# Softmax with temperature: from eight small tile buffers to a ring of large blocks with a row maximum

## The chip, the cores and the metric

The kernel runs on one core of a Trainium2 chip. The metric is the device time of one execution in microseconds (us), lower is better. Before the change, ten runs have a median of 319.7 us and lie between 319.55 and 319.8.

Five engines matter for reading it. ACT (ScalarE) computes exponentials, DVE (VectorE) reduces and multiplies, SP (SyncE) only issues transfers, and PE and POOL do next to nothing here. Transfers between the chip's main memory (HBM) and its on-chip memory (SBUF, 128 partitions) are issued from the queue of an engine (SP's and ACT's in this case) and carried by 16 DMA engines.

## The reference

`x` is 32 x 512 x 1024 float32, 67.1 MB. The temperature is 0.5.

```python
scaled = x / temperature
shifted = scaled - np.max(scaled, axis=-1, keepdims=True)
exp_x = np.exp(shifted)
return (exp_x / np.sum(exp_x, axis=-1, keepdims=True)).astype(np.float32)
```

It is a softmax over rows of 1024 elements, and there are 16384 rows. All of `x` must be read once and all of the result written once, 134.2 MB together.

## The kernel before, in words

The rows are taken 512 at a time: 128 partitions, with K = 4 consecutive rows in each. One such tile is 2 MiB, 16 KiB in each partition, and the four rows of a partition lie next to each other in HBM too. There are 32 tiles, and one loop goes over them (`for it, (g0, K) in enumerate(sched)`). A pool of eight buffers (`data`) holds the tiles; a tile is computed in place, so its buffer is taken from the start of its load to the end of its store.

For each tile the loop issues, in this order:

- the load, from SP's queue (line 47);
- four exponentials on ACT (line 52), one per row of the partition. Each computes exp(scale * x) and also leaves the sum of its row in `sums`. The maximum is not subtracted;
- one reciprocal of the four sums on DVE (line 59);
- four multiplications on DVE (line 61), each with its row's reciprocal;
- the store, from ACT's queue (line 70). For the last four tiles the store is cut in two halves, one from ACT's queue (line 67) and one from SP's (line 68).

The waits are not written out. The tile framework derives them from the buffers: a load waits for the store of the tile that had its buffer eight tiles earlier, an exponential waits for the load, a reciprocal for the exponentials, a store for the multiplications. Each engine works through its own instructions in program order, so SP's queue holds 32 loads with the four last half stores behind them, and ACT's queue holds the exponentials with the stores between them. The store of tile n stands in ACT's queue where the loop puts it, three exponentials into the next tile (the compiler's order), so that ACT need not stand still for DVE.

Of the kernel before, what the change touches and what calls it, by code (L numbers as in the profile page):

```python
# [1 line left out]

# [4 lines left out]


@with_exitstack  # L10
def kernel(
    ctx: ExitStack,
    tc: tile.TileContext,
    x: bass.AP,
    temperature: bass.AP,
    out: bass.AP,
):
    nc = tc.nc
    scale = 1.0 / float(temperature)

    P = 128
    xf = x.flatten_outer_dims()
    of = out.flatten_outer_dims()
    n, d = xf.shape
    nrowgroups = n // P

    K_MAIN = 4
    SPLIT_LAST = 4
    sched = []
    g = 0  # L30
    while g < nrowgroups:
        k = min(K_MAIN, nrowgroups - g)
        sched.append((g, k))
        g += k
    ntiles = len(sched)

    data = ctx.enter_context(tc.tile_pool(name="data", bufs=8))
    stats = ctx.enter_context(tc.tile_pool(name="stats", bufs=16))

    for it, (g0, K) in enumerate(sched):  # L40
        rows = P * K
        r0 = g0 * P
        xv = xf[r0 : r0 + rows, :].rearrange("(p k) d -> p (k d)", p=P, k=K)
        ov = of[r0 : r0 + rows, :].rearrange("(p k) d -> p k d", p=P, k=K)

        xtile = data.tile([P, K, d], mybir.dt.float32)
        nc.sync.dma_start(out=xtile.rearrange("p k d -> p (k d)"), in_=xv)  # L47

        sums = stats.tile([P, K], mybir.dt.float32)
        recip = stats.tile([P, K], mybir.dt.float32)  # L50
        for j in range(K):
            nc.scalar.activation(  # L52
                xtile[:, j, :],
                xtile[:, j, :],
                mybir.ActivationFunctionType.Exp,
                scale=scale,
                accum_out=sums[:, j : j + 1],
            )
        nc.vector.reciprocal(recip, sums)  # L59
        for j in range(K):  # L60
            nc.vector.tensor_scalar_mul(  # L61
                xtile[:, j, :], in0=xtile[:, j, :], scalar1=recip[:, j : j + 1]
            )

        if it >= ntiles - SPLIT_LAST and K > 1:
            h = K // 2
            nc.scalar.dma_start(out=ov[:, :h, :], in_=xtile[:, :h, :])  # L67
            nc.sync.dma_start(out=ov[:, h:, :], in_=xtile[:, h:, :])
        else:
            nc.scalar.dma_start(out=ov, in_=xtile)  # L70


# [1 line left out]
_INS = ['x', 'temperature']  # L74
_OUTS = [((32, 512, 1024), 'float32')]
#: Inputs that are plain numbers.
_NUMBERS = {'temperature': 0.5}


# [26 lines left out]
```

## Time and profile before

| | |
|---|---|
| median of 10 runs | 319.7 us |
| the profiled execution's own time | 320.02 us |
| its span in the profile | 318.1 us |
| ACT busy | 138.0 us (43%) |
| DVE busy | 93.4 us (29%) |
| exponential, 128 x 1024, line 52 | 128 times, mean 1044 ns |
| multiplication, 128 x 1024, line 61 | 128 times, mean 749 ns |
| reciprocal, 128 x 4, line 59 | 32 times, mean 178 ns |
| bytes moved | 67.11 MB read, 67.11 MB written, mean 422 GB/s |
| load of 2 MiB, issue to landing | median 31.2 us, least 7.8 us |
| store of 2 MiB from ACT's queue, issue to landing | median 24.3 us |

The span is what the profiler sees between the first and the last instruction; the time of an execution is some 1.9 us longer, and the profiled execution is itself 0.3 us above the median. Busy times are sums over one execution. In the row of 40 digits each digit is the busy share of one fortieth of the span (about 8 us), in tenths. The chain that ended last is followed back from the end: at each step to what released the waiting work. A line of the windows table gives a stretch in us from the span's start, its length, the busy time and number of instructions of DVE, ACT and POOL, the granted TensorE clock, the DMA engines' busy share, and the rate in GB/s. A line of the waits gives who waited for what, and then the total in us, how many times, and the longest.

### The profile page before, as it was taken

The numbers are of one execution on the slowest core, as the hardware profiler recorded it, in microseconds if no ns is written. First come the engines' busy times: TensorE is split into PE (matmuls) and PEld (weight loads), VectorE is DVE, ScalarE is ACT, GpSimd is POOL, SyncE is SP. The second block draws the span as 40 slices with busy tenths as digits, with TensorE's granted clock in tenths as the row PEclk, the third lists the DMA queues.
The fourth block names the chain that finished last, engine by engine and source line by source line (L and its number), as shares of the span: only waits on it lengthen the run. The fifth ranks groups of instructions, "written<-read, shape, count | busy, mean of one in ns | idle before, by whom it ended". The sixth has DMA issues, their size and how long they took to land.

```text
span 318.1 us, 636 instructions
## 1 busy us (share of the span) xinstructions
DVE 93.4 (29%) x160; ACT 138.0 (43%) x257; POOL 0.2 (0%) x4
## 2 busy tenths in 40 slices
DVE  0352333212300517631333213333123003733300
ACT  1875334553321739655334553345543106852500
POOL 0000000000000000000000000000000000000000
DMA  8999999999999999999999999999999999999996
GB/s 291 433 398 429 429 429 428 431 429 439 433 437 433 428 431 429 429 429 431 429 431 434 437 433 433 431 429 431 429 429 431 429 433 433 439 433 419 427 427 265
DMA packets 9797, 134.26 MB, mean 422 GB/s; under 512 B 1088, under 2 KB 1088, under 8 KB 1088
## 3 DMA queue, kind: packets, MB, share of 16 engines
q1 hardware_dynamic: 5184, 71.31, 52.9%
q10 hardware_dynamic: 4608, 62.92, 46.2%
q14 instruction: 5, 0.04, 0.0%
HBM read 67.11 MB, written 67.11 MB: 422 GB/s over the span
## 4 chain that ended last, share of the span: by engine, by line
DMA 91%; ACT 1%; SPq 1%; DVE 1%; issue 0%; DVEq 0%; ACTq 0%
DMA xtile<-in_x_dram 55%; DMA out_dram<-xtile 36%; ACT xtile L52 1%; SPq L47 1%; DVE xtile L61 1%; DVEq L101 0%; ACTq L67 0%; DVE recip L59 0%; ACTq L52 0%; ACTq L70 0%
## 5 line engine op out<-in xcount | busy, mean ns | idle before, releaser
L52 ACT ACTIVATE xtile<-xtile 128x1024 f32<-128x1024 f32 x128 | 133.6, 1044 | 159.6 <-DMA xtile<-in_x_dram 158.4
L61 DVE TENSOR_SCALAR xtile<-xtile,recip 128x1024 f32<-128x1024 f32 x128 | 87.7, 749 | 1.1
L59 DVE RECIPROCAL recip<-sums 128x4 f32<-128x4 f32 x32 | 5.7, 178 | 206.7 <-ACT xtile L52 206.7
L52 ACT ACTIVATION_READ_ACCUMULATOR xtile<-xtile 128x1 f32 x128 | 23.9, 187 | 0.0
L52 ACT ACT_TABLE_LOAD x1 | 1.3, 1283 | 0.7 <-PEq L87 0.7
L87 POOL MEMSET const-bfloat16-1.0<- 128x1 bf16 x1 | 0.1, 101 | 0.0
L87 POOL MEMSET const-uint8-127<- 128x1 uint8 x1 | 0.1, 101 | 0.0
L87 POOL MEMSET const-float32-0.0<- 128x1 f32 x1 | 0.1, 98 | 0.2 <-issue 0.2
L87 POOL MEMSET const-float32-1.0<- 128x1 f32 x1 | 0.1, 98 | 0.0
## 6 DMA issues: line engine op xcount, KB each, us to landing
xtile<-in_x_dram SPq DMA_DIRECT2D x32, 2048.0 KB, 31.2
out_dram<-xtile ACTq DMA_DIRECT2D x28, 2048.0 KB, 24.3
out_dram<-xtile ACTq DMA_DIRECT2D x4, 1024.0 KB, 22.8
out_dram<-xtile SPq DMA_DIRECT2D x4, 1024.0 KB, 14.9
```

The source lines that it names most:

```text
L47: nc.sync.dma_start(out=xtile.rearrange("p k d -> p (k d)"), in_=xv)
L52: nc.scalar.activation(xtile[:, j, :], xtile[:, j, :], mybir.ActivationFunctionType.Exp, scale=scale, accum_out=sums[:, j : j + 1],)
L59: nc.vector.reciprocal(recip, sums)
L61: nc.vector.tensor_scalar_mul(xtile[:, j, :], in0=xtile[:, j, :], scalar1=recip[:, j : j + 1])
L87: nc = _bacc.Bacc("TRN2", target_bir_lowering=False, num_devices=1)
```

## The change

The kernel's loop is replaced by lists that are written out by hand, and the framework's waits by semaphores (counters on which an engine can wait).

- **Blocks.** Nine loads in place of 32: seven of 16 rows per partition (8 MiB, 64 KiB in each partition) and two of 8 rows (4 MiB). Ten stores in place of 36: six of 16 rows, four of 8.
- **Ring.** One buffer of 48 rows per partition (192 KiB), in which blocks 0 to 8 lie at rows 0, 16, 32, 0, 16, 32, 0, 16 and 24. A load waits for the store of what lay in its place: loads 3, 4, 5, 6 wait for stores 0, 1, 2, 3, and loads 7 and 8 both for store 4. A semaphore for each load and each store carries these waits.
- **Row maximum.** For each group of four rows per partition DVE finds the maxima (one reduction of 128 x 4 x 1024, line 91) and multiplies them by minus the scale (line 101); the exponential on ACT (line 109) takes the result as its bias.
- **Order on DVE.** For g from 0 to 32: maximum and bias of group g, then reciprocal (line 122) and four multiplications (line 128) of group g - 1. So the last group of a block is multiplied behind the maximum of the next block's first group.
- **Order on ACT.** The exponentials of group g, then a store (line 149) if group g - 1 was the last of one. The store waits for that group's multiplications.
- **Order on SP.** The nine loads (line 142), then waits for the stores that are left. No store is issued from SP any more.

```diff
+LOADS = [16] * 7 + [8] * 2
+STORES = [[16]] * 6 + [[8, 8]] + [[8]] * 2
+RING = 48
+GROUP = 4
...
-    data = ctx.enter_context(tc.tile_pool(name="data", bufs=8))
-    stats = ctx.enter_context(tc.tile_pool(name="stats", bufs=16))
...
-        nc.sync.dma_start(out=xtile.rearrange("p k d -> p (k d)"), in_=xv)
...
-        nc.vector.reciprocal(recip, sums)
-        for j in range(K):
-            nc.vector.tensor_scalar_mul(
-                xtile[:, j, :], in0=xtile[:, j, :], scalar1=recip[:, j : j + 1]
...
+    def maximum(g):
+        i, s, r, k = groups[g]
+        if g == 0 or groups[g - 1][0] != i:
+            nc.vector.wait_ge(loaded[i], 16)
+        nc.vector.tensor_reduce(
+            out=top[:, r : r + k],
+            in_=ring[:, s : s + k, :],
+            axis=mybir.AxisListType.X,
+            op=extreme,
+        ).then_inc(topped, 1)
+
+    def shift(g):
+        i, s, r, k = groups[g]
+        nc.vector.wait_ge(topped, g + 1)
+        nc.vector.tensor_scalar_mul(
+            bias[:, r : r + k], in0=top[:, r : r + k], scalar1=-scale
+        ).then_inc(biased, 1)
+
+    def exponential(g):
+        i, s, r, k = groups[g]
+        nc.scalar.wait_ge(biased, g + 1)
+        for a in range(k):
+            ins = nc.scalar.activation(
+                ring[:, s + a, :],
+                ring[:, s + a, :],
                 mybir.ActivationFunctionType.Exp,
+                bias=bias[:, r + a : r + a + 1],
                 scale=scale,
-                accum_out=sums[:, j : j + 1],
+                accum_out=sums[:, r + a : r + a + 1],
             )
+        ins.then_inc(summed, 1)
...
+    def load(i):
+        nonlocal free_to
+        s, r, k = places[i], first[i], LOADS[i]
+        for n, (l, s1, r1, k1) in enumerate(parts):
+            if l < i and s1 < s + k and s < s1 + k1 and n > free_to:
+                for b in range(free_to + 1, n + 1):
+                    nc.sync.wait_ge(stored[b], 16)
+                free_to = n
+        nc.sync.dma_start(out=ring[:, s : s + k, :], in_=dram(xf, r, k, i)).then_inc(
+            loaded[i], 16
+        )
+
+    def store(n):
+        l, s, r, k = parts[n]
+        nc.scalar.wait_ge(scaled, part_end[n])
+        nc.scalar.dma_start(out=dram(of, r, k, l), in_=ring[:, s : s + k, :]).then_inc(
+            stored[n], 16
+        )
+
+    free_to = -1
+    with tc.tile_critical():
+        for i in range(len(LOADS)):
+            load(i)
+        for b in range(free_to + 1, len(parts)):
+            nc.sync.wait_ge(stored[b], 16)
+
+        for g in range(len(groups) + 1):
+            if g < len(groups):
+                exponential(g)
+            for n in range(len(parts)):
+                if part_end[n] == g:
+                    store(n)
+
+        for g in range(len(groups) + 1):
+            if g < len(groups):
+                maximum(g)
+                shift(g)
+            if g > 0:
+                invert(g - 1)
+                divide(g - 1)
```

`invert` and `divide` are the reciprocal and the four multiplications of a group, on the ring's rows, with a wait on `summed` and on `inverted` ahead of them and an increment of `scaled` behind the last.

## The prediction

> **What bounds the kernel now.** I read the page's head and slices first, then the chain that ended last, then the queue's own waits, then short windows at both ends. Head, slices and queues:
>
> ```profile
> span 318.1 us, 636 instructions
> DVE 93.4 (29%) x160; ACT 138.0 (43%) x257; POOL 0.2 (0%) x4
> ...
> DMA  8999999999999999999999999999999999999996
> ...
> HBM read 67.11 MB, written 67.11 MB: 422 GB/s over the span
> ```
>
> No engine is half busy, but the DMA engines are full in every slice between the first and the last. The chain agrees: nine tenths of it is DMA.
>
> ```profile
> DMA 91%; ACT 1%; SPq 1%; DVE 1%; issue 0%; DVEq 0%; ACTq 0%
> DMA xtile<-in_x_dram 55%; DMA out_dram<-xtile 36%; ACT xtile L52 1%; SPq L47 1%; DVE xtile L61 1%; DVEq L101 0%; ACTq L67 0%; DVE recip L59 0%; ACTq L52 0%; ACTq L70 0%
> ```
>
> So the time is bytes over rate. 134.2 MB in some 310 us is about 430 GB/s, and windows show that rate whether loads run alone (8 to 16 us), both kinds run (128 to 192), or stores run alone (304 to 312):
>
> ```profile
> 8.00:16.00 8.00, 2.92 (x5) 6.85 (x13) 0.00 (x0) 1.00 1.00 430
> ...
> 128.00:192.00 64.00, 21.65 (x38) 30.28 (x58) 0.00 (x0) 1.00 1.01 432
> ...
> 304.00:312.00 8.00, 0.00 (x0) 0.00 (x0) 0.00 (x0) 1.00 1.01 429
> ```
>
> In the trace's packet records a 16 KiB packet takes 611 ns on its engine and an 8 KiB one 309 ns: 7 ns for the packet itself plus 604 ns per 16 KiB. Each engine carries 480 and 64 of them: 480 x 0.611 + 64 x 0.309 = 313.1 us. The other 5 us of the span are start and end. The only way to be slower is to leave the DMA engines empty. The queue's waits say how near that is:
>
> ```profile
> SPq L47 <- DMA out_dram<-xtile: 228.7, 24, 17.0
> ```
>
> Loads already wait for stores to free buffers, all the time, and it costs nothing: eight 16 KiB buffers mean that when one store lands, others are still in flight. What a transfer costs on an **empty** queue is seen only at the start. The first load is issued at 0.73, and the first bytes move after 1.7:
>
> ```profile
> 1.50:1.70 0.20, 0.00 (x0) 0.20 (x1) 0.00 (x0) 1.00 0.00 0
> 1.70:1.90 0.20, 0.00 (x0) 0.20 (x1) 0.00 (x0) 1.00 2.71 573
> ...
> 0.00:8.00 8.00, 0.00 (x0) 1.28 (x1) 0.20 (x4) 1.00 0.81 293
> ...
> DMA to landing us min/median/max: 7.8/31.2/48.4
> ```
>
> That is 1.0 us from issue to first byte. By 8.0 us 2.34 MB have moved, 5.45 us at 430 GB/s, so the effective start is 2.55: 0.8 us more are lost while the flow builds up. And that load took 7.8 us to land for 8 x 0.611 = 4.9 us of packets: 2.9 us of fixed cost on the slowest engine, of which about 0.35 lies after its last packet.
>
> **What the Trainium skill says.** "DMA: Bandwidth & Descriptors", section "Issuing engines are not separate DMA queues": SP's and ACT's transfers interleave on the same 16 engines; the windows agree (430 alone, 432 together). Same page, "Queues, rings and completion order": each engine serves the queues in turn, packet by packet; I take it that a load and a store in flight together get half each, which no row here shows singly. Same page, "Anatomy of one DMA": waits are held by the issuing sequencer, so a queue whose next transfer is unissued has nothing to run. "VectorE: DVE Perf Modes", the perf-mode tier table: a reduction handles one element per cycle; its price is below.
>
> **The change, part by part.**
>
> *Row maximum and bias.* 32 reductions of 128x4096 and 32 tiny multiplications are added on DVE. No such row exists. The skill's page gives about 150 fixed cycles and 0.96 GHz: (4096 + 150) / 0.96 = 4.42 us, an estimate; its other figure, 58 cycles, gives 4.33. The kernel's own multiplication has a pitch of 0.685 us for 1024 elements at two per cycle, which 150 fits ((512 + 150) / 0.96 = 0.69) and 58 does not; I take 4.45 with the wait, bounds 3.5 and 5.5. The small operations cost 0.2 each, as the reciprocal's step does (12.81 to 13.02). A group of four rows now costs DVE 4.45 + 0.2 + 0.2 + 2.75 (four multiplications, 13.02 on) = 7.6 us, in total 243 us instead of 93. This stays under the 9.7 us of transfers per group, so it does not bound by rate, but it sits in every buffer's round trip. ACT's work per group stays 4.16 us (four at a 1.04 pitch; its bias is taken at nothing, since ACT has 3 us to spare per group).
>
> *Longer transfers.* A partition's run grows from 16 to 64 KiB. If packets grow with it, an engine has 7 x 8 + 2 x 8 load packets and 6 x 8 + 4 x 8 store packets, 152 instead of 544: 392 x 7 ns = 2.7 us saved. If they don't, 0. I take 2.7.
>
> *Stores behind the next group.* The last multiplication of a block stands on DVE behind the maximum of the **next** block's first group, which waits for that block's load. So store n needs load n+1 landed plus 4.65 + 2.95 + 0.3 = 7.9 us. ACT's wait on the multiplications stands behind that group's exponentials and ahead of the next group's; DVE finishes about 3 us after ACT was released, ACT needs 4.2, so it costs nothing.
>
> *The ring.* Three 8 MiB blocks instead of eight of 2 MiB, and load n+3 waits for the whole of store n. A block is 8 packets of 2.42 us per engine, 19.4 us alone, 38.8 us when it shares with another. The walk, by hand:
>
> Load 0 lands at 22.5 (issued at 0.95, 0.2 later than now for the entry of the ordered section, + 1.0 + 0.8 + 19.4 + 0.35), the others by 61. Store 0 needs five maxima and four groups' multiplications: 22.5 + 5 x 4.65 + 4 x 2.95 = 57.6. Later blocks follow at 4 x 7.6 = 30.4 us: store 1 at 88.3 (with some 0.3 for hand-over). But store 0, which shares only with load 2's rest, is through at 80.3. **First gap**: nothing is in flight, load 3 is issued at 80.7, first byte 1.0 later, 0.8 to build up: 2.2 us. Load 3 then leads store 1 by 6.8 us; both finish their 38.8 us at 121.3, the load ahead, landed at 114.4. Store 2 is issued 7.9 later, 122.3; store 1 has already ended. **Second gap.** The rule: a round has a gap unless the load leads its store by 7.9 + 1.0 = 8.9 us or more. Walked on like this, the leads of the four rounds behind store 1 to store 4 come out as 6.8, about 0, 4.6 and 2.2 us, so with the first there are five dry ends (stores 0 to 4, at 80, 121, 162, 203, 244 us). From 245 on loads and stores of eight rows overlap; the last store is issued near 310 while the one before runs to 314.5, so the tail adds nothing.
>
> A gap costs 2.2 us by the mean over engines, 2.9 if the slowest engine pays in full, 1.4 if the build-up belongs to the program's start only. I take 2.3. **Sum: 318.1 + 5 x 2.3 - 2.7 = 326.9 us of span.** Fewer issues (19 for 68, 0.33 us each) were hidden behind full queues and count nothing. The profiled execution took 320.02, 1.9 above its span; the median shown, 319.7, is 1.6 above. With 1.6: **328.5 us**. With 1.4 per gap 324.0; with 2.9 and no packet saving 334.2.
>
> **Rivals.** (1) *Fewer gaps*: round 1 is only 2.1 us from the lead that closes its gap, so a different start could break the pattern. With two gaps: 318.1 + 4.6 - 2.7 + 1.6 = 321.6. Against: the first gap has 8 us of margin, and each later one is followed by a load and store starting nearly together. (2) *No gaps, faster*: if the reduction ran at two elements per cycle, (150 + 2048) / 0.96 = 2.3 us, a block would take 21.8 us, store 1 would be out before store 0 is through, and only the packet saving remains: 318.1 - 2.7 + 1.6 = 317.0. It decides at a reduction of about 3.2 us; the page's one element per cycle speaks against it. (3) *DVE becomes the bound*: at 6.5 us per maximum a group costs 9.7, and waiting for loads and computing no longer overlap; the same walk ends at 346, time 347.6. It begins to hurt from 5.5 (333 of span). Nothing in the trace shows DVE slowed by ACT or DMA. (4) *Long rows move slower*: 2% on the packets is 6.3 us: with the gaps but no saving, 318.1 + 11.5 + 6.3 + 1.6 = 337.5. The trace has only 8 and 16 KiB, where longer was better.
>
> **How the numbers follow.** Five gaps 0.70, fewer gaps 0.12, none 0.07, DVE bound 0.07, slow rows 0.04. The range 322 to 335 spans the likeliest case with its bounds and most of rival 1; rivals 2, 3 and 4, 0.18 together, lie outside. Only rival 2 is faster by over 0.2% (0.6 us, about what a measurement of this kernel can tell from no change); a single gap would be near no change (0.02).
>
> **What would show it.** The slices' DMA row should dip near 80, 121, 162, 203 and 244 us, each time with SP released by a store and no store queued; the maximum's row should read 4.3 to 4.6 us, DVE about 240 busy; packets in q1 should fall to some 1,300. The prediction is wrong if a store is out before the one ahead of it ends, or if the maximum is under 3.2 or over 5.5 us.

## The result, and the profile after

The changed kernel takes 337.5 us (median of 8 runs, 336.58 to 338.16) against 319.7 for the kernel before (28 runs): a ratio of 1.0555, 95% interval 1.0546 to 1.0565. It is slower by 17.9 us. The forecast was slower by 8.8, so its direction was right and its size was not; 337.5 lies above the range. The profiled execution's span is 335.5 us.

The head, the slices and the queues of the page after:

```profile
span 335.5 us, 554 instructions
DVE 234.9 (70%) x224; ACT 149.6 (45%) x257; POOL 0.2 (0%) x4
...
DMA  9898989898798959999698988989988998999996
...
q1 hardware_dynamic: 1296, 67.11, 49.4%
...
HBM read 67.11 MB, written 67.11 MB: 400 GB/s over the span
```

The bytes are the same, the mean rate fell from 422 to 400 GB/s. The loads' queue has 1296 packets, so they did grow with the partition's run. The row of digits shows less than one expects: a slice is 8.4 us long, a dry stretch of under 2 us only turns a 9 into an 8 or 7, and since a slice counts a packet where it starts, packets of 2.4 us make the digits jump by themselves. Two views are sharper. The first is SP's own waits: five times a load stood waiting for a store, 249 us in all.

```profile
SPq L142 <- DMA out_dram<-ring: 248.9, 5, 80.3
```

The second is a set of short windows of the changed kernel, laid where those five waits end (columns: stretch in us, its length, busy time and instructions of DVE, ACT and POOL, clock, DMA share, GB/s):

```profile
82.20:83.50 1.30, 1.30 (x1) 0.00 (x0) 0.00 (x0) 1.00 0.00 0
124.80:125.90 1.10, 1.06 (x3) 1.08 (x2) 0.00 (x0) 1.00 0.00 0
167.20:168.40 1.20, 1.20 (x1) 0.00 (x0) 0.00 (x0) 1.00 0.16 55
209.50:210.70 1.20, 1.17 (x4) 1.04 (x1) 0.00 (x0) 1.00 0.00 0
252.20:253.40 1.20, 1.20 (x1) 0.00 (x0) 0.00 (x0) 1.00 0.00 0
```

In all five the DMA engines stand still, but for first packets at the end of the third, while DVE works. (A window, too, counts a packet where it starts; the trace's packet records show that none from before is still in service.) The walk had them at 80, 121, 162, 203 and 244; the lag grows from 2 to 8 us. The rows of the three large groups of instructions:

```profile
L109 ACT ACTIVATE ring<-ring,bias 128x1024 f32<-128x1024 f32 x128 | 145.4, 1137 | 165.3 <-DVE bias L101 165.3
L91 DVE TENSOR_REDUCE top<-ring 128x4 f32<-128x4096 f32 x32 | 141.3, 4415 | 79.6 <-DMA ring<-in_x_dram 79.6
L128 DVE TENSOR_SCALAR ring<-ring,recip 128x1024 f32<-128x1024 f32 x128 | 87.7, 749 | 1.1
```

The reduction takes 4.415 us and DVE waits 79.6 us for loads: DVE is not the bound, it stands in the round trip.

### The profile page after: what moved, and what is told of

It reads as the page before. It is cut to its first block, busy times and chain, and to the rows that moved or that the text cites. A ratio compares the mean times of both kernels' runs of the same rounds, so it can differ in the third digit from the quotient of the medians.

```text
span 335.5 us, 554 instructions
## 1 busy us (share of the span) xinstructions
DVE 234.9 (70%) x224; ACT 149.6 (45%) x257; POOL 0.2 (0%) x4
## 3 DMA queue, kind: packets, MB, share of 16 engines
q1 hardware_dynamic: 1296, 67.11, 49.4%
## 4 chain that ended last, share of the span: by engine, by line
DMA 74%; DVE 15%; ACT 5%; issue 0%; SPq 0%
DMA ring<-in_x_dram 43%; DMA out_dram<-ring 31%; DVE top L91 10%; ACT ring L109 5%; DVE ring L128 4%; DVE bias L101 0%; DVE recip L122 0%; SPq L142 0%; SPq L206 0%; SPq L154 0%
## 5 line engine op out<-in xcount | busy, mean ns | idle before, releaser
L109 ACT ACTIVATE ring<-ring,bias 128x1024 f32<-128x1024 f32 x128 | 145.4, 1137 | 165.3 <-DVE bias L101 165.3
L91 DVE TENSOR_REDUCE top<-ring 128x4 f32<-128x4096 f32 x32 | 141.3, 4415 | 79.6 <-DMA ring<-in_x_dram 79.6
L128 DVE TENSOR_SCALAR ring<-ring,recip 128x1024 f32<-128x1024 f32 x128 | 87.7, 749 | 1.1
L109 ACT ACTIVATION_READ_ACCUMULATOR ring<-ring,bias 128x1 f32 x128 | 23.9, 187 | 0.0
L101 DVE TENSOR_SCALAR bias<-top 128x4 f32<-128x4 f32 x32 | 5.4, 170 | 1.1
```

What stands on the lines that cost most here:

```text
L91: nc.vector.tensor_reduce(out=top[:, r : r + k], in_=ring[:, s : s + k, :], axis=mybir.AxisListType.X, op=extreme,).then_inc(topped, 1)
L101: nc.vector.tensor_scalar_mul(bias[:, r : r + k], in0=top[:, r : r + k], scalar1=-scale).then_inc(biased, 1)
L109: ins = nc.scalar.activation(ring[:, s + a, :], ring[:, s + a, :], mybir.ActivationFunctionType.Exp, bias=bias[:, r + a : r + a + 1], scal ...
L128: ins = nc.vector.tensor_scalar_mul(ring[:, s + a, :], in0=ring[:, s + a, :], scalar1=recip[:, r + a : r + a + 1])
```

## Where the time went

The windows say that the queues run dry, not what it costs. That can be worked out from the trace's packet records: add up what all packets have moved by some moment, divide by the full rate, and subtract from the clock. In the changed kernel a 64 KiB packet takes 2.418 us on one of 16 engines, so the full rate is 433.6 GB/s, and 134.2 MB need 309.5 us of it. The rest of the 335.5 is lost time, and it grows only in a few places:

```
changed kernel, time lost against the full rate (us)
until 8       2.7    start
58 to 64      1.4    the first store enters beside the loads
81 to 95      4.0    store 0 has ended, load 3 starts, store 1 enters
124 to 136    3.7    store 1, load 4, store 2
166 to 180    3.8    store 2, load 5, store 3
209 to 222    3.7    store 3, load 6, store 4
251 to 266    4.0    store 4, loads 7 and 8, store 5
to the end    2.6    last store's packets and landing
sum          25.9    = 335.5 - 309.5, rounded
```

Five dry ends cost 19.2 us, **3.85 each** (3.7 to 4.0). Within one the loss has three parts. The first is idle time, 1.85 on average (1.7 to 2.0), from the moment when an engine ends its packets, by the mean of the 16, to the first packet of the load: the last engine ends 0.4 to 0.6 later, SP issues the load 0.35 to 0.5 after that, and the first packet starts 0.95 after the issue. The other two parts are 2.0 us together in all five: **0.8** while the load's first packets take longer than 2.418, and **1.2 when the store enters** (it is issued 2.7 to 5.1 us after the load): each load packet then in service takes up to 4 us. In the rounds that begin at 124 and 209 us the two parts run into each other, and only their sum can be read.

Windows show it for the first dry end, where each engine starts one packet in each stretch: the load's first, its second, its third, and the store's first.

```profile
83.45:86.35 2.90, 2.83 (x7) 2.50 (x5) 0.00 (x0) 1.00 1.03 362
86.35:88.80 2.45, 2.45 (x2) 2.14 (x4) 0.00 (x0) 1.00 0.99 428
88.80:92.55 3.75, 3.68 (x5) 1.31 (x3) 0.00 (x0) 1.00 0.99 280
92.55:94.95 2.40, 2.40 (x4) 2.40 (x5) 0.00 (x0) 1.00 1.01 437
```

The engines' share stays full in the third stretch while the rate falls to 280 GB/s.

## The experiments

**Smaller blocks.** All blocks 8 rows per partition, so that the ring has six places; everything else, the maximum included, stays.

```diff
-LOADS = [16] * 7 + [8] * 2
-STORES = [[16]] * 6 + [[8, 8]] + [[8]] * 2
+LOADS = [8] * 16
+STORES = [[8]] * 16
```

> The changed kernel with all blocks of 8 rows per partition: 16 loads and 16 stores, six places of 32 KiB per partition in the ring instead of three of 64 KiB. Theory A (three large places and a compute path in every round trip let both queues run dry five times): with six places the next store is always issued before the one ahead ends, so no gap and one entry of the store queue; span 317 to 319, time 318.5 to 320.5. Theory B (the row maximum on DVE costs the time): still 335 or more. Theory C (packets of more than 16 KiB cost the time): about half of the loss stays, 326 to 330.

Measured: 318.8 us, 0.9975 of the kernel before (0.9966 to 0.9985), span 317.0. Its page:

```profile
span 317.0 us, 568 instructions
DVE 235.5 (74%) x224; ACT 149.6 (47%) x257; POOL 0.2 (0%) x4
...
DMA  8999999999999999999999999999999999999994
...
L91 DVE TENSOR_REDUCE top<-ring 128x4 f32<-128x4096 f32 x32 | 141.3, 4416 | 62.9 <-DMA ring<-in_x_dram 62.9
```

DVE does as much as in the changed kernel, and between start and end only the first store's entry loses time, 0.7 us by the packet records: no slice between first and last is below 9. SP waits for stores nearly as long as in the changed kernel, 225 us, and it is free, since three or four other blocks are on their way each time. So the loss comes with the size of the blocks relative to the ring; that it is not the length of the packets is shown further down (Short packets). This version is 0.25% faster than the kernel before, which is small, but the interval leaves out 1.

**Blocks of four rows.** The block size of the kernel before, with the changed code.

```diff
+LOADS = [4] * 32
+STORES = [[4]] * 32
+RING = 32
```

> The changed kernel's code with the block size of the kernel before: 32 loads and 32 stores of 4 rows per partition, ring of eight 16 KiB places, the maximum kept. Theory A: no dry end, one entry, packets of 16 KiB; within 0.3% of the kernel before, 319 to 320.5, and some 1 us above the blocks of 8. If the maximum or the hand-written order costs anything by itself: above 322.

Measured: 320.0 us, ratio 1.0009 (1.0001 to 1.0018), span 318.2. The maximum and the hand-written order together cost some 0.3 us, by the interval at most 0.6, where queues stay full. Blocks of 8 are 1.2 us below. That fits their packets: between 40 and 310 us the packet records show 432.8 GB/s with blocks of 8 and 431.0 with blocks of 4, which is 1.3 us on 134.2 MB.

**No maximum.** The reduction and the bias are left out, and ACT waits for the load itself.

```diff
-        nc.scalar.wait_ge(biased, g + 1)
+        if g == 0 or groups[g - 1][0] != i:
+            nc.scalar.wait_ge(loaded[i], 16)
...
-                maximum(g)
-                shift(g)
```

> The changed kernel without the row maximum and the bias (the maximum is not subtracted, as in the kernel before); blocks, ring, packets and semaphores stay. Theory A: a store leaves some 12 us earlier, the five gaps close, but a store still enters beside a running load each round, 5 or 6 entries of 1.2 us; time 322 to 326. Theory B: all of the loss goes, 318 to 320. Theory D (the ring of three places alone, whatever is computed): 333 or more.

Measured: 329.7 us, ratio 1.0300 (1.0266 to 1.0334), span 328.6. None of the three theories had this. With DVE busy for 93.4 us instead of 234.9 the large blocks still cost 10 us. The packet records show why the expectation was low: the dry ends are gone (between 5 and 320 us there is no moment when all engines stand still; in the changed kernel there are 6.8 us of such moments), but in each round a load and a store are still issued within 3 us of each other, beside the end of a transfer, and packets are slow there: 0.9 to 2.9 us lost each time, near 87, 125, 161 to 175, 202 to 212, 250 and 273 us. The end costs 4.8 us, against 2.6 in the changed kernel. So taking the maximum away gives back 8 of the 18 us, and 10 stay with the large blocks. The maximum costs only together with them: the blocks of 8 keep it and lose next to nothing.

**Multiplications first.** The last group of each block is multiplied ahead of the next block's first maximum, and its store goes ahead of the next block's exponentials. This undoes the part of the order that makes a store need the next load.

```diff
+            ends = 0 < g < len(groups) and groups[g][0] != groups[g - 1][0]
+            if ends:
+                invert(g - 1)
+                divide(g - 1)
             if g < len(groups):
                 maximum(g)
                 shift(g)
-            if g > 0:
+            if g > 0 and not ends:
...
```

(This is the part on DVE; the one on ACT, which puts the store ahead of the exponentials, is left out here.)

> The changed kernel with the last group of each block multiplied ahead of the next block's first maximum on DVE, and its store ahead of the next block's exponentials on ACT; all else stays. Theory A, by the walk: a store no longer needs the next load, so only the first gap (near 82 us) stays; 3 or 4 entries; time 321 to 326. If the order on DVE doesn't matter: 336 to 339.

Measured: 325.3 us, ratio 1.0188 (1.0153 to 1.0222), within what the walk gave. One full dry end stays, at 82 us; the windows of this kernel show it, and behind it the load's slow first packets and the slow ones at the store's entry:

```profile
82.60:83.30 0.70, 0.00 (x0) 0.70 (x2) 0.00 (x0) 1.00 0.00 0
83.40:86.30 2.90, 2.83 (x5) 0.01 (x1) 0.00 (x0) 1.00 1.07 362
88.75:92.50 3.75, 3.71 (x3) 1.54 (x3) 0.00 (x0) 1.00 0.99 280
```

Then nothing is lost from 95 to 200 us. Smaller losses follow near 206 (1.9, where load 6 and store 4 start together) and near 310 (1.7, a hole between two late stores). So another order at the blocks' ends gives back 12 of the 18 us. This and the 8 us of the run before are no shares of a whole: each is what one edit gives back, and they overlap.

**Halved stores.** Only the stores of the large blocks are cut; the loads keep 16 rows.

```diff
+STORES = [[8, 8]] * 7 + [[8]] * 2
```

> The changed kernel with every store of 16 rows cut in two of 8 (loads, ring, order and the maximum stay; packets of stores 32 KiB). A block's first half leaves two groups, 15 us, earlier, so that the second half follows it without a break. Theory A: no dry end except perhaps the first, entries of a store beside a load stay where the halves leave a hole; time 321 to 327. If a dry queue is not what costs: 335 or more.

Measured: 319.3 us, ratio 0.9990 (0.9982 to 0.9998), better than expected. Of its page:

```profile
span 317.5 us, 565 instructions
...
DMA  9999989989998999999799999999999999999995
```

A half block leaves 15 us earlier, and the second half follows before the first has ended, so ACT's queue never empties after the first store. The loads then enter beside running stores four times and lose little (0.0 to 0.3 us each). One constant takes back all that the change had cost.

**Three dry ends instead of five.** The first three blocks' stores halved, the others whole.

```diff
+STORES = [[8, 8]] * 3 + [[16]] * 3 + [[8, 8]] + [[8]] * 2
```

> The changed kernel with the stores of the first three blocks cut in halves and the others left whole. By the walk two of the five dry ends go and three stay (ends of the whole stores). Theory A with 3.85 us for a dry end: 337.5 - 2 x 3.85 = 329.8, between 328 and 332. If a dry end costs only the 2.3 us of the prediction: 332.9 or more.

Measured: 331.9 us, ratio 1.0378 (1.0361 to 1.0395), span 330.4: inside the range given, and less of a gain (5.6 us) than 2 x 3.85. The packet records show three dry ends, at 161, 204 and 247 us, with 4.3, 4.1 and 3.9 lost. Of the remaining 2 us, 1.3 are at the end, where this execution's engines finish further apart (3.9 us from full rate to the end of the span, against 2.6 in the changed kernel), and 0.7 lie in the three dry ends, each a little dearer than 3.85. The price of a dry end is confirmed within 0.4 us, the sum to 2 us.

**Short packets.** Loads and stores cut into transfers of four rows with the same waits, so that packets are 16 KiB. The loads' part of the edit:

```diff
-        nc.sync.dma_start(out=ring[:, s : s + k, :], in_=dram(xf, r, k, i)).then_inc(
-            loaded[i], 16
-        )
+        for c in range(0, k, 4):
+            nc.sync.dma_start(
+                out=ring[:, s + c : s + c + 4, :], in_=dram(xf, r + c, 4, i)
+            ).then_inc(loaded[i], 16)
```

> The changed kernel with every load and store cut into transfers of 4 rows per partition, so that packets are 16 KiB again; blocks, ring, waits and order stay (a block's parts count on one semaphore). Theory A: five gaps stay; 2.5 us more for packets, up to 3 us less if an entry costs 0.7 us as with the kernel before's packets; time 336 to 340. Theory C: 322 to 328.

Measured: 336.5 us, ratio 1.0526 (1.0512 to 1.0541). The long packets are neither the cause nor much of a help: the five dry ends stay, at some 3.5 us each. The store's entry within them takes 0.7 to 0.8 us where it stands apart, so packet length sets part of its size; what is saved there pays for the lower rate of the short packets.

**What an entry costs.** In these probes nothing is computed: loads fill a ring that no one reads, and stores write a constant tile to part of the output. Each pair moves the same bytes with many entries of the store queue or with one.

```diff
+        for i in range(LOADS):
+            if i >= AHEAD:
+                nc.sync.wait_ge(loaded[i - AHEAD], 16)
+            nc.sync.dma_start(out=ring[:, s : s + ROWS, :], in_=...).then_inc(loaded[i], 16)
+        for j, i in enumerate(STORE_AFTER):
+            nc.scalar.wait_ge(loaded[i], 16)
+            nc.scalar.dma_start(out=..., in_=fixed[:STORE_P]).then_inc(stored[j], 16)
```

> A probe that computes nothing: 32 loads of 2 MiB run without a break from SP's queue, and ten stores of 2 MiB of a constant tile leave ACT's queue one at a time, three loads apart, so that ACT's queue is empty before each. Packets are 16 KiB. If a queue's entry beside a running one costs 0.7 us (read from the kernel before, 391 GB/s in 16 to 24 us), this takes 9 x 0.7 = 6 us more than the same bytes with one entry (next run). If entries are free: the same time.

> The same bytes, but the ten stores are issued one behind the other: one entry. 88.1 MB at 434 GB/s is 203 us; span some 208 us.

Measured: 212.6 and 213.2 us. By the packet records the first store's entry loses 0.6 us (0.7 in the burst); the other nine, each into an empty store queue, lose nothing. With long packets:

> The same probe with packets of 64 KiB: 8 loads of 8 MiB without a break, and seven stores of 2 MiB (32 partitions of 64 KiB) one at a time, one load apart. If an entry costs 1.2 us with such packets (read from the changed kernel), 6 x 1.2 = 7 us more than the next run; if it costs the same as with 16 KiB, 4 us more.

> The same bytes as the run before it with the seven stores one behind the other: one entry. 81.8 MB at 434 GB/s is 189 us; span some 194 us.

Measured: 216.1 and 213.4 us, and this pair settles nothing: the spans, 214.8 and 211.3, are 21 and 17 us above the 194 expected, with slow packets beside the stores and engines that finish up to 17 us apart at the end. A store from 32 of the 128 partitions is a different transfer from the kernel's. The pair was repeated with stores from all partitions:

> A probe that computes nothing: 8 loads of 8 MiB with the load queue never empty, and three stores of 8 MiB of a constant tile (128 partitions of 64 KiB), each entering ACT's empty queue beside a running load. If every entry beside a running load costs 1.2 us with such packets: 2.4 us more than the next run, and each entry seen in the trace. If an entry costs only at first or after both queues ran dry: the same time as the next run, and only the first entry seen.

> The same bytes with the three stores one behind the other: one entry. 92.3 MB at 434 GB/s is 213 us; span some 218 us.

Measured: 221.2 and 223.4 us; the one with more entries is the faster. Its first entry loses 0.9 us, its second nothing, its third 0.6. So an entry has no fixed price, and the last question was what sets it.

**Dry or not.** Two more probes of this kind, with a delay on DVE, so that each store is issued about 6 us after a load has landed. They differ in one number: whether a second load is in flight.

```diff
-AHEAD = 2
+AHEAD = 1
```

> A probe that computes nothing: 8 loads of 8 MiB, each issued only when the one before has landed, so that the queues run dry seven times; 6 us after each landing a store of 4 MiB of a constant tile enters beside the load just started. If the slow entry belongs to the dry end: each of the seven entries loses about 1.2 us, besides about 2.7 us for each dry end. 96.5 MB at 434 GB/s is 222.5 us, plus 5 for start and end, plus 7 x 3.9: span 255. If entries are free here too: 246.

> The same probe with two loads in flight, so that the load queue never runs dry; the stores enter at the same moments. If the slow entry belongs to the dry end: only the first entry loses about 1 us, span some 229. If every entry of a store costs 1.2 us: seven times, span 236.

Measured: 243.7 us with one load in flight (r_dry) and 231.1 with two (r_wet), spans 243.0 and 229.4. Loss around each store's entry, from the packet records:

```
entry of store   1      2      3      4      5      6      7
r_wet           0.95   0.00   0.00   0.00   0.00   0.00   0.00
r_dry           0.85   0.25   1.25   1.0    0.7    0.9    0.95
```

The table looks as if the slow entry belonged to the restart of the loads, but the pair differs in more than was meant. In r_wet each store after the first was issued some 6 us before the store ahead of it had ended (store 1 at 54.5, store 0 ended at 60.2), so ACT's queue was not empty, and there was no entry to price. In r_dry ACT's queue was empty each time. And its queues were both dry only once: in the six later rounds the store still ran for 2.0 to 3.3 us when the next load was issued, which is also why its span fell short of the 255 expected. What r_dry shows by itself is that a store which enters an empty queue some 6 us after a load was issued lost 0.7 to 1.25 us in six rounds of seven.

For the restart as the cause there is one comparison with packets of equal length, 16 KiB: in p16_spaced nine stores enter an empty queue beside loads that never pause and lose nothing, in the changed kernel with short packets they enter beside a load just restarted and lose 0.7 to 0.8. The two differ in other things too, so this cause is likely but not shown.

## Why the prediction was wrong in size

- *What bounds the kernel.* Right: DMA at its full rate with no gap sets the time of the kernel before. That "the only way to be slower is to leave the DMA engines empty" was not: some 1.2 us of each dry end, and most of the 10 us that stay without the maximum, are lost while the engines are busy, by packets that take longer.
- *Maximum at 4.45 us, 7.6 us of DVE for a group.* Right: 4.415, and groups follow each other at 7.39. The single rate that the Trainium skill gives a reduction ("VectorE: DVE Perf Modes", the perf-mode tier table) holds here: the estimate from it was 4.42.
- *ACT's bias at nothing.* Right for the path, wrong as a fact: an exponential with a bias from memory takes 1137 ns instead of 1044. ACT had the room.
- *Packets grow, 2.7 us saved.* Right, to 0.3. By the lengths of the packets it would be 3.4: 104 x 2.418 + 48 x 1.213 = 309.7 us for each engine instead of 313.1. But in the kernel before an engine's packets overlap a little in the records: from 24 to 312 us it moved 430.7 GB/s, where 0.611 us for 16 KiB gives 429. With the rates measured after, 434.2 with 64 KiB and 433.3 with 32, the saving is 2.4.
- *A load and a store in flight together get half each.* Taken on trust, and about right: between 135 and 158 us 77 load packets and 80 store packets start.
- *Five dry ends.* Right in number and place. Store 1 was issued at 86.7 (walk 88.3), load 3 at 82.5 (80.7), store 2 at 127.7 (122.3). Loads 3 to 6 were issued 4.2, 2.7, 5.1 and 2.7 us ahead of stores 1 to 4, all far from the 8.9 that would have closed a gap, so that five was no luck.
- **"A gap costs 2.2 us ... I take 2.3": this is the term that failed.** A gap cost 3.85. The idle part came out at 1.85 where the prediction had 1.4 (0.4 for the landing, 1.0 to the first byte): these two were right, but the engines end apart, and by their mean that adds some 0.5. The build-up of 0.8 was right. The store's entry beside the restarted load, 1.2 us, was not in the sum at all. 5 x (3.85 - 2.3) = 7.75 us, of the 8.6 by which the span (335.5 against 326.9) was missed. The first store's entry, 1.4 us where the kernel before has 0.6, adds 0.8; the smaller saving on packets adds 0.3; start and end give 0.3 back.

The missing part could have been read from the kernel before. There the first store enters beside running loads at about 19 us, and these lines were in reach:

```profile
16.00:24.00 8.00, 4.29 (x8) 5.95 (x12) 0.00 (x0) 1.00 1.00 391
24.00:32.00 8.00, 1.95 (x5) 4.26 (x8) 0.00 (x0) 1.00 1.00 426
```

391 instead of 430 GB/s over 8 us is 0.7 us. It happens once in that kernel, and I took no note of it; in the changed kernel each round starts afresh and pays it again, with the longer packets at 1.2 us.

The rivals: no gaps, a DVE bound and slow long rows are refuted by the windows, by DVE's 79.6 us of waiting and by the 2.418 us packet. That slow long rows were priced at 337.5, the very time measured, is chance: a 64 KiB packet moves no slower than four of 16 KiB. Fewer gaps did not happen, and when the runs made them fewer, the time fell.

## What to carry to other kernels

A transfer-bound kernel is limited by its buffers' granularity as much as by their bytes: with three large places a load must wait for exactly the store that nothing covers, while six half-size places in the same memory lost 0.7 us at the first store and nothing behind it. When a queue can run dry, price the whole restart, not only the issue: here 1.85 us still, 0.8 us to build up, 1.2 us when the other queue joins. And it can be enough to cut the transfer whose end releases the next one: here halving the stores alone gave back 18 us.

## What the runs showed that was not expected

- A store that enters an empty queue beside running loads can be free: nine of nine entries after the first in p16_spaced, where the loads never pause. In the changed kernel, where the load has just been restarted, it costs about 1.2 us. The DMA engines' share reads as full in that time, because packets are longer, not absent. What decides stays open: entries some 6 us behind a load's issue lost between 0.25 and 1.25 us in r_dry, one entry of q64_spaced lost 0.6 without a restart, and the first store of a run lost 0.2 to 1.4 us beside loads that had run without a break. Packet length changes how much is lost (0.7 to 0.8 us with 16 KiB at a restart), but not whether.
- Without the maximum the large blocks still lose 10 us with hardly a moment of idle engines. Slow packets near starts, and a longer end, account for it in the records; why they are more there than in the halved stores' kernel, which starts loads beside running stores too, was not tried.
- With stores from 32 partitions, 64 KiB each, 17 and 21 us were lost on 82 MB: some 11 us by packets that took longer than 2.418 us, the rest by engines that ran out of work one after another. Why was not tried.
